# Recurrent mixer: V's second tile and token shift placed behind the keys, and the low-rank weights loaded ahead of V's

## The chip, the core and the metric

The kernel runs on one core of a Trainium2 chip. The core has five engines with queues of their own: TensorE (PE, with its weight loads shown as PEld), VectorE (DVE), ScalarE (ACT), GpSimd (POOL) and SyncE (SP, which here only issues DMAs). Each queue is worked off in order, and instructions wait for other engines on semaphores. The metric is the device time of one execution in microseconds.

## The reference

Two layers on 256 tokens of width 1024. Each layer is a SwiGLU block, a mixer and a second SwiGLU block, each between two RMS norms. Layer 0 has the mixer in question, layer 1 an attention mixer. What matters here, cut from the reference:

```python
p = proj[..., :COLS_RWKV]
p_prev = jnp.pad(p, ((0, 0), (1, 0), (0, 0)))[:, :-1]
p = p + shift_mu * (p_prev - p)                     # token shift
r, k, v, d_w, d_a, d_g = split_cols(p, [...])
decay = exp(-exp(-softplus(-(decay_base + tanh(d_w) @ decay_up)) - 0.5))
a = sigmoid(iclr_base + d_a @ iclr_up)              # low-rank parts
g = sigmoid(d_g) @ gate_up
kk = normalised(k * k_k);  k = k * (1 + (a - 1) * k_a)
# per token: S = S diag(w) - (S kk)(kk a)^T + v k^T ;  y = S r
y_b = silu(layer_norm(conv(c_val * sigmoid(c_gate)) + conv_b))
return concat([y_a, y_b]) @ w_out
```

## The kernel before

All tokens are held as two tiles of 128 (t = 0, 1). Every float32 product is made of three passes with operands split into a high and a low part. A weight page of 128x1024 floats is loaded by SP into one of 10 `raw` buffers; `split` (L97) then casts it on ScalarE into `whi` (L98) and forms `wlo = raw - whi` on VectorE or, for the names in `POOLED` (among them `av`, `alora`, `ak`, `ar`, `ao0`), on GpSimd (L99). There are 8 `whi` and 8 `wlo` buffers; a page is taken in the order in which `plan` (L1034) has added it.

The stages are SwiGLU, recurrent mixer, two SwiGLUs, attention, SwiGLU. The recurrent mixer, `mixer_a` (L564), calls its parts in the order of the letters in `ORDER` (L22), "VLDKPQkRIBCcbA2nS". Those that matter here:

- V, `values` (L603): for each token tile the product with `av` (24 matmuls 128x512, by `xunit`, L338), its scaling into `pv` on ScalarE (L615), and DMAs from ScalarE's queue that copy `pv` down by one row into `prev` (L618, L620). Between the tiles `across` (L377) makes `rb`, the row scale for products that stand transposed. Then, for each tile, the token shift on GpSimd (L622 to L624), the mean over 64 columns on VectorE (L626, L627) and its subtraction into `vz` on GpSimd (L630). `vz` is first read by the state stage.
- L, `lora` (L641): the product with `alora` (48 matmuls 128x256, by `wunit`, L352), its shift (`shifted`, L632: `n` on VectorE at L635, ScalarE at L638, VectorE at L639), tanh and sigmoid, and the small products that give `sg`, `ic` and `gg`.
- D, `decay` (L667): `restart` set by GpSimd (L671, L672), a scan on VectorE (L674), `epx` on GpSimd (L676), exponentials on ScalarE.
- K, `keys` (L661): two products of 48 matmuls and their shift. P, Q: `bk`, `ur` and the matrix `Q` (L730, 16 instructions on VectorE).
- I, `invert` (L732): `Q` goes to DRAM and back (L740, L746), a chain of small VectorE instructions inverts 16x16 blocks (L749 to L773), and the results go to DRAM and back as `G` and `T`.
- C, `glu` (L834): two gated products; `z` on VectorE (L845), its sigmoid on ScalarE (L846), `glu` on VectorE (L847). c, `conv`: diagonal weights `dw` on ScalarE (L906), taps on VectorE (L926, `feed`), on GpSimd (L915) and on TensorE (`pfeed`, `gu<-glu,dw`).
- A, 2, S: `ak` and `ar` (L818, L821), the doubling of `G` and `T`, and the state over four chunks.

This call order sets priorities; the order on each engine is laid down by a scheduler when the kernel is built. `issue_after` keeps an instruction behind another in that order.

Of the kernel before, what the change touches and what calls it, by code (L numbers as in the profile page):

```python
# [12 lines left out]
ALU = mybir.AluOpType  # L13
PSUM = bass.MemoryType.PSUM
P = 128
D = 1024
# [2 lines left out]
TAG = dict(sq8="y2", qn="yc", gz="z", fz="tmp", fe="c16", fl="lora", fc="n", fraw="restart", pt="yb", y="muv",  # L19
           cb="ur", cbm="bk", gt="sg", qt="ic", kt="k", v="vz", y0="ar")  # L20

ORDER = "VLDKPQkRIBCcbA2nS"  # L22

NRAW, NWEIGHT, NAHEAD = 10, 8, 8

# [67 lines left out]
class Kernel:  # L93
# [470 lines left out]
    def mixer_a(self, j, rstd, nxt, then):  # L564
        nc, W, a = self.nc, self.w, self.a
        V = nc.vector
# [15 lines left out]
        m = {}  # L582
# [8 lines left out]
        muv = self.temp("muv", [512])  # L591
# [11 lines left out]
        def values():  # L603


            vz = m["vz"] = [half(self.page("vz")) for _ in range(2)]
            pv, prev = m["v"], _ = half(self.page("pv")), half(self.page("prev"))
            W.upto(("av",))
            with self.tc.issue_after(self.pow.ins):
                nc.gpsimd.memset(prev[0:1, 0, :], 0.0)  # L610
            for t in range(2):
                if t:
                    m["rb"] = self.across(rstd)
                ps = self.xunit(("av",), t)
                nc.scalar.activation(pv[:, t, :], ps, AF.Copy, scale=rstd[t])  # L615

                for a, b in ((0, 112), (112, P - 1)):
                    nc.scalar.dma_start(out=prev[a + 1:b + 1, t, :], in_=pv[a:b, t, :])  # L618
                if t == 0:
                    nc.scalar.dma_start(out=prev[0:1, 1, :], in_=pv[P - 1:P, 0, :])  # L620
            for t in range(2):
                nc.gpsimd.tensor_tensor(out=prev[:, t, :], in0=prev[:, t, :], in1=pv[:, t, :], op=ALU.subtract)  # L622
                m["shift"] = nc.gpsimd.tensor_tensor(out=prev[:, t, :], in0=prev[:, t, :], in1=muv, op=ALU.mult)
                nc.gpsimd.tensor_tensor(out=pv[:, t, :], in0=prev[:, t, :], in1=pv[:, t, :], op=ALU.add)  # L624
                v8 = self.small("v8", 8)
                V.tensor_reduce(out=v8, in_=h8(pv[:, t, :]), axis=AX.X, op=ALU.add)  # L626
                V.tensor_scalar(out=v8, in0=v8, scalar1=1.0 / 64, scalar2=None, op0=ALU.mult)  # L627
                for c in range(2):
                    cs = slice(64 * c, 64 * c + 64)
                    nc.gpsimd.tensor_tensor(out=h8(vz[t][cs, c, :]), in0=h8(pv[cs, t, :]), in1=v8[cs].unsqueeze(2).broadcast_to([64, 8, 64]), op=ALU.subtract)  # L630
# [36 lines left out]
        def decay():  # L667
            sg = m["sg"]
            restart = self.temp("restart", [1024], BF16)
            with self.tc.issue_after(m["shift"].ins):  # L670
                nc.gpsimd.memset(restart, 1.0)  # L671
                nc.gpsimd.memset(restart.rearrange("p (n t) -> p n t", t=64)[:, :, 0:1], 0.0)  # L672
            dc = self.page("dc")
            V.tensor_tensor_scan(out=dc, data0=restart, data1=flat(sg), initial=0.0, op0=ALU.mult, op1=ALU.add)  # L674
            epx = self.page("epx")
            nc.gpsimd.tensor_tensor(out=epx, in0=dc, in1=flat(sg), op=ALU.subtract)  # L676
            nc.scalar.activation(epx, epx, AF.Exp, scale=-DEC)
            ep = self.page("ep")
            nc.scalar.activation(ep, dc, AF.Exp, scale=-DEC)
            nc.scalar.activation(dc, dc, AF.Exp, scale=DEC)  # L680
            m["epx"], m["ep"], m["en"] = grp(epx), grp(ep), grp(dc)
# [286 lines left out]
        def state():  # L968
# [4 lines left out]
            for ch in range(4):  # L973
# [44 lines left out]
                    ts = slice(t * P, (t + 1) * P)  # L1018
                    self.split(self.xth[:, 0:4, ts], self.xtl[0][:, :, ts], tp.rearrange("p (g t) -> p g t", t=P))

        f = {"V": values, "L": lora, "K": keys, "D": decay, "P": prep, "k": kprep, "Q": qmats, "I": invert, "R": receptance, "A": amats,
             "B": kback, "C": glu, "2": doubling, "b": bonus, "c": conv, "n": convend, "S": state}
        for z in ORDER:
            f[z]()
# [9 lines left out]
    def plan(self, stages):  # L1034
        W, a = self.w, self.a
        flat = lambda ap: ap.rearrange("p k f -> p (k f)")
        for st in stages:
            if st in "0134":
                j = int(st)
                l, f = j // 3, j % 3  # L1040
                units = self.units()
                for i, u in enumerate(units + [None] * 2):
# [7 lines left out]
                    if i >= 2:  # L1050
                        v = units[i - 2]
# [1 line left out]
                            if ("d", j, v[1], k) not in W.where:  # L1053
                                W.add(("d", j, v[1], k), a["wd"][l, f, v[1], :, k], 1024)
            if st == "A":
                for name in [n for z in ORDER for n in dict(V=["av"], L=["alora"], K=["ak"], R=["ar"], C=["acv", "acg"]).get(z, [])]:
                    if name == "av":
                        for h in range(2):
                            W.add((name,), flat(a["av"][h]), 512)
                        continue  # L1060
                    o, n = {"ak": (0, 4), "ar": (4, 4), "acv": (8, 4), "acg": (12, 4), "alora": (16, 2)}[name]
                    for g in range(o, o + n):
                        W.add((name,), flat(a["ain"][g]), 128)
                for h in (2, 3, 0, 1):
                    W.add(("ao", h // 2), flat(a["aout"][h]), 1024)
# [10 lines left out]
    def run(self, out):  # L1076
        tc, nc, a = self.tc, self.nc, self.a
        self.turn = 0
        with tc.tile_pool(name="c", bufs=1) as c, tc.tile_pool(name="raw", bufs=NRAW) as raw, tc.tile_pool(name="pg") as pg, \
# [26 lines left out]
            nc.sync.dma_start(out=self.x[1], in_=a["x"][P:2 * P, :])  # L1106
            order = "0A13C4"
            rstd = {t: self.pre(t, order.index(self.stages[0])) for t in range(2)}
            first = lambda st: {"A": [("av",), ("alora",)], "C": [("q", 0), ("k", 0)]}.get(st) or [("g", int(st), 0), ("g", int(st), 1)]
            for n, st in enumerate(self.stages):  # L1110
                nx = self.stages[n + 1] if n + 1 < len(self.stages) else None
                f = getattr(self, {"A": "mixer_a", "C": "mixer_c"}.get(st, "ffn"))
# [85 lines left out]
```

## Time and profile before

| what | value |
| --- | --- |
| three runs | 1122.84, 1125.05, 1146.17 us; median 1125.05 us |
| the profiled execution | 1123.03 us, of which 1121.2 us is the span from first to last instruction |
| busy in the span | PE 96%, PEld 84%, DVE 60%, ACT 51%, POOL 23% |
| the recurrent mixer | from about 207 us to about 386 us of the span |

A row of the timeline reads: start and duration in us, engine, line, operation, output<-inputs, count, and in brackets how long the engine had been idle before it and what ended that. "SPq" and "ACTq" are a queue's DMA issues. In a list of waits the columns are the engine and line that waited, whom it waited for, us in total, number of times and the longest. A row of the stretches gives the busy time of each engine in it, the TensorE clock that was granted (1.00 is 2.4 GHz, 0.50 is 1.2 GHz), the busy share of the DMA engines and GB/s.

### The profile page before, as it was taken

Reading aid. Unit: us, or ns where it says so; the run is one execution under the profiler, and the core shown is the slowest. Engines: PE = TensorE matmul, PEld = TensorE weight load, DVE = VectorE, ACT = ScalarE, POOL = GpSimd, SP = SyncE. Lnnn points to the kernel's source line nnn. Section 1 sums busy time; section 2 is a strip of 40 time slices with the busy share of each in tenths; the row PEclk is TensorE's granted clock in tenths of the full one; section 3 lists DMA queues with packets and bytes.
Section 4 is the critical chain, followed back from the end, with each engine's and each line's share of the span. In section 5 each row is a group of like instructions: output and inputs, shape, how many; then the busy total and the mean of one; then the engine's idle time right before and its main releaser. Section 6 shows DMA issues by size and latency. Waiting matters only on the chain.

```text
span 1121.2 us, 17652 instructions
## 1 busy us (share of the span) xinstructions
PE 1075.6 (96%) x6955; PEld 947.1 (84%) x6955; DVE 668.3 (60%) x1064; ACT 568.5 (51%) x933; POOL 255.1 (23%) x194
## 2 busy tenths in 40 slices
PE   7999999999698899999989999999999989999997
PEld 5899998889587789999878999988887868999986
DVE  4465661599887556547444555836667665555722
ACT  7444553673453464446354544634666945444611
POOL 4200006571662170000070000001564540000000
PEclk9999999998798999999999999999999999999999
DMA  9766785245410246557554464744273553765400
GB/s 361 246 212 185 235 308 177 86 165 151 104 39 1 76 151 244 201 189 271 168 186 151 167 227 170 240 138 151 90 286 107 193 189 101 226 193 179 148 1 37
DMA packets 65321, 189.27 MB, mean 169 GB/s; under 512 B 18360, under 2 KB 19672, under 8 KB 65238
## 3 DMA queue, kind: packets, MB, share of 16 engines
q1 hardware_dynamic: 55386, 186.18, 49.4%
q10 hardware_dynamic: 9852, 1.96, 1.0%
q8 instruction: 54, 0.88, 0.3%
q14 instruction: 29, 0.24, 0.1%
HBM read 184.68 MB, written 2.92 MB: 167 GB/s over the span
## 4 chain that ended last, share of the span: by engine, by line
PE 66%; DVE 7%; ACT 2%; DMA 1%; issue 1%; POOL 1%; ACTq 0%; DVEq 0%; POOLq 0%
PE gu L352 23%; PE acc L263 16%; PE gu L223 12%; PE gu L338 5%; PE acc L370 3%; PE gu L585 2%; PE acc L585 2%; DVE cv L926 2%; DVE wlo L99 1%; DVE x L148 1%; PE tr L158 1%; POOL p L484 1%; PE tr L506 1%; ACT whi L98 0%; DMA raw<-in_cout_dram 0%
## 5 line engine op out<-in xcount | busy, mean ns | idle before, releaser
L98 ACT CAST whi<-raw 128x1024 fp32r<-128x1024 f32 x294 | 303.4, 1047 | 206.2 <-PE gu L352 110.8
L99 DVE TENSOR_TENSOR wlo<-raw,whi 128x1024 fp32r<-128x1024 f32 x248 | 312.5, 1266 | 133.9 <-ACT whi L98 108.1
L352 PE MATMUL gu<-xth,wlo 128*128 128x256 f32 x1104 | 314.1, 284 | 0.0
L352 PE MATMUL gu<-xl,whi 128*128 128x256 f32 x1104 | 313.1, 284 | 0.0
L352 PE MATMUL gu<-xth,whi 128*128 128x256 f32 x1104 | 313.1, 284 | 0.0
L352 PEld LDWEIGHTS gu<-xth,wlo 128*128 128x128 f32 x1104 | 212.0, 192 | 3.5 <-issue 0.9
L352 PEld LDWEIGHTS gu<-xth,whi 128*128 128x128 f32 x1104 | 211.8, 192 | 3.3 <-issue 0.7
L352 PEld LDWEIGHTS gu<-xl,whi 128*128 128x128 f32 x1104 | 211.9, 192 | 1.0 <-issue 0.8
L99 POOL TENSOR_TENSOR wlo<-raw,whi 128x1024 fp32r<-128x1024 f32 x46 | 113.9, 2506 | 300.1 <-PE gu L223 141.5
L263 PE MATMUL acc<-whi,ht 128*128 128x512 f32 x576 | 168.0, 393 | 0.0
L113 POOL TENSOR_TENSOR misc<-misc 128x1 f32<-128x1 f32 (+1 forms) x36 | 31.6, 880 | 476.0 <-DVE misc L130 380.7
L263 PEld LDWEIGHTS acc<-whi,ht 128*128 128x128 f32 x576 | 104.0, 189 | 18.3
L263 PE MATMUL acc<-wlo,ht 128*128 128x512 f32 x288 | 89.9, 392 | 0.0
L234 DVE TENSOR_TENSOR h<-gu,h 128x256 f32<-128x256 f32 x88 | 36.9, 420 | 77.9 <-ACT h L230 74.7
L232 DVE TENSOR_TENSOR h<-gu,misc 128x256 f32<-128x256 f32 x56 | 23.7, 424 | 80.1 <-PE gu L352 80.1
L223 PE MATMUL gu<-whi,xth 128*128 128x512 f32 x160 | 63.8, 403 | 1.8 <-ACT whi L98 1.8
L223 PE MATMUL gu<-wlo,xth 128*128 128x512 f32 x160 | 64.0, 400 | 0.5 <-DVE wlo L99 0.5
L263 PEld LDWEIGHTS acc<-wlo,ht 128*128 128x128 f32 x288 | 53.9, 188 | 11.8
L223 PE MATMUL gu<-whi,xl 128*128 128x512 f32 x160 | 63.3, 400 | 0.1
L233 ACT ACTIVATE h<-h 128x256 f32<-128x256 f32 x56 | 23.2, 415 | 53.7 <-DVE h L232 53.7
L230 ACT ACTIVATE h<-gu,misc 128x256 f32<-128x256 f32 x32 | 15.1, 475 | 66.9 <-PE gu L223 36.9
L338 PE MATMUL gu<-whi,xth 128*128 128x512 f32 x112 | 44.9, 401 | 1.1 <-ACT xth L162 0.9
(254 smaller groups left out, 1589.6 us busy)
## 6 DMA issues: line engine op xcount, KB each, us to landing
raw<-in_wgc_dram SPq DMA_DIRECT2D x112, 512.0 KB, 4.5
raw<-in_wd_dram SPq DMA_DIRECT2D x88, 512.0 KB, 4.7
raw<-in_wgt_dram SPq DMA_DIRECT2D x64, 512.0 KB, 5.3
raw<-in_cin_dram SPq DMA_DIRECT2D x24, 512.0 KB, 5.2
raw<-in_ain_dram SPq DMA_DIRECT2D x18, 512.0 KB, 4.5
raw<-in_aout_dram SPq DMA_DIRECT2D x8, 512.0 KB, 5.1
raw<-in_cgate_dram SPq DMA_DIRECT2D x8, 512.0 KB, 7.5
raw<-in_cout_dram SPq DMA_DIRECT2D x8, 512.0 KB, 3.7
```

The lines of the kernel that those rows point to most:

```text
L98: self.nc.scalar.copy(out=hi, in_=raw)
L99: (engine or self.nc.vector).tensor_tensor(out=lo, in0=raw, in1=hi.bitcast(F32), op=ALU.subtract)
L113: self.pow = self.nc.gpsimd.tensor_tensor(out=out, in0=v, in1=self.mhalf[:, :n], op=ALU.pow)
L223: nc.tensor.matmul(ps, lhsT=l, rhs=r[:, k % 2], start=n == 0, stop=n == 23)
L232: nc.vector.tensor_tensor(out=z, in0=ps[:, 0:256], in1=self.rb, op=ALU.mult)
L233: nc.scalar.activation(sl, z, AF.Silu)
L234: nc.vector.tensor_tensor(out=h, in0=ps[:, 256:512], in1=sl, op=ALU.mult)
L263: mm = nc.tensor.matmul(out, lhsT=l, rhs=r, start=u[1] == 0 and i + n == 0, stop=u[1] == NB - 1 and i * 3 + n == 5)
L338: self.nc.tensor.matmul(ps, lhsT=l, rhs=r[:, k % 2], start=n == 0, stop=n == 23)
L352: self.nc.tensor.matmul(ps[:, j * 256:(j + 1) * 256], lhsT=l, rhs=r, start=n == 0, stop=n == 23)
L370: self.nc.tensor.matmul(accs[t][c], lhsT=l, rhs=r[:, 0, c * 512:(c + 1) * 512], start=k == ks[0] and n == 0, stop=k == ks[7] and n == 2)
L585: return nc.tensor.matmul(out, lhsT=lhsT, rhs=rhs, start=start, stop=stop, skip_group_check=True)
```

## The change

V's first tile, with `across`, stays where it was. The product of the second tile and the whole token shift become a part of its own, "v", called behind P. The pages of `alora` are planned, and taken at the end of the SwiGLU before, ahead of those of `av`. `restart` is held only behind the last `pow` of the norm, no longer behind the shift. Lines behind L611 move by about five.

```diff
-ORDER = "VLDKPQkRIBCcbA2nS"
+ORDER = "VLDKPvQkRIBCcbA2nS"
...
-            for t in range(2):
-                if t:
-                    m["rb"] = self.across(rstd)
+
+            def product(t):
                 ps = self.xunit(("av",), t)
                 nc.scalar.activation(pv[:, t, :], ps, AF.Copy, scale=rstd[t])
...
+            product(0)
+            m["rb"] = self.across(rstd)
+            m["rest"] = lambda: (product(1), shift_values(vz, pv, prev))
+
+        def shift_values(vz, pv, prev):
             for t in range(2):
                 nc.gpsimd.tensor_tensor(out=prev[:, t, :], in0=prev[:, t, :], in1=pv[:, t, :], op=ALU.subtract)
-                m["shift"] = nc.gpsimd.tensor_tensor(out=prev[:, t, :], in0=prev[:, t, :], in1=muv, op=ALU.mult)
+                nc.gpsimd.tensor_tensor(out=prev[:, t, :], in0=prev[:, t, :], in1=muv, op=ALU.mult)
...
-            with self.tc.issue_after(m["shift"].ins):
+            with self.tc.issue_after(self.pow.ins):
                 nc.gpsimd.memset(restart, 1.0)
...
-        f = {"V": values, "L": lora, ...
+        f = {"V": values, "v": lambda: m["rest"](), "L": lora, ...
...
-                for name in [n for z in ORDER for n in dict(V=["av"], L=["alora"], K=["ak"], R=["ar"], C=["acv", "acg"]).get(z, [])]:
+                for name in [n for z in ORDER for n in dict(V=["alora", "av"], K=["ak"], R=["ar"], C=["acv", "acg"]).get(z, [])]:
...
-            first = lambda st: {"A": [("av",), ("alora",)], "C": [("q", 0), ("k", 0)]}.get(st) or [("g", int(st), 0), ("g", int(st), 1)]
+            first = lambda st: {"A": [("alora",), ("av",)], "C": [("q", 0), ("k", 0)]}.get(st) or [("g", int(st), 0), ("g", int(st), 1)]
```

The orders differ only inside the recurrent mixer (and in three places of SP's loads around it). At its start TensorE had, behind the transposes of the second token tile (`x_75`), V's second product (L338) interleaved with the low-rank product (L352):

```order
L158 MATMUL tr<-cst,x_75 128x128 x8
L338 MATMUL gu<-whi,xth 128x512
L338 MATMUL gu<-wlo,xth 128x512
L352 MATMUL gu<-xth,whi 128x256
L352 MATMUL gu<-xth,wlo 128x256
L338 MATMUL gu<-whi,xl_88 128x512
L352 MATMUL gu<-xl_88,whi 128x256
L338 MATMUL gu<-whi,xth 128x512
```

Now the low-rank product stands there alone:

```order
L158 MATMUL tr<-cst,x_75 128x128 x8
L352 MATMUL gu<-xth,whi 128x256
L352 MATMUL gu<-xth,wlo 128x256
L352 MATMUL gu<-xth,whi 128x256
L352 MATMUL gu<-xth,wlo 128x256
L352 MATMUL gu<-xl_88,whi 128x256 x2
```

V's 24 matmuls come behind both products of the keys. On GpSimd, at the same place, the row was this before; `wlo` are weight pages, `prev`, `pv` and `vz` the shift of V's tiles:

```order
L610 MEMSET prev 1x512
L622 TENSOR_TENSOR prev<-prev,pv 128x512
L623 TENSOR_TENSOR prev<-prev,muv 128x512
L99 TENSOR_TENSOR wlo<-raw,whi 128x1024
L624 TENSOR_TENSOR pv<-prev,pv 128x512
L99 TENSOR_TENSOR wlo<-raw,whi 128x1024 x2
L630 TENSOR_TENSOR vz<-pv,misc 64x512 x2
L99 TENSOR_TENSOR wlo<-raw,whi 128x1024 x2
L622 TENSOR_TENSOR prev<-prev,pv 128x512
L99 TENSOR_TENSOR wlo<-raw,whi 128x1024
L623 TENSOR_TENSOR prev<-prev,muv 128x512
L671 MEMSET restart 128x1024
```

and is this now:

```order
L610 MEMSET prev 1x512
L676 MEMSET restart 128x1024
L677 MEMSET restart 128x16
L627 TENSOR_TENSOR prev<-prev,pv 128x512
L628 TENSOR_TENSOR prev<-prev,muv 128x512
L629 TENSOR_TENSOR pv<-prev,pv 128x512
L635 TENSOR_TENSOR vz<-pv,misc 64x512 x2
L99 TENSOR_TENSOR wlo<-raw,whi 128x1024 x5
L681 TENSOR_TENSOR epx<-dc,sg 128x1024
L99 TENSOR_TENSOR wlo<-raw,whi 128x1024
L627 TENSOR_TENSOR prev<-prev,pv 128x512
L628 TENSOR_TENSOR prev<-prev,muv 128x512
```

The first tile's shift is done in one go ahead of the weight pages, the second tile's stands behind `epx`. On VectorE, at the end of `Q`, the row was

```order
L730 SCALAR_TENSOR_TENSOR Q<-acc_2417,misc,cst 128x64
L730 SCALAR_TENSOR_TENSOR Q<-acc_2418,misc,cst 128x64
L635 TENSOR_TENSOR n<-gu,misc 128x512
L99 TENSOR_TENSOR wlo<-raw,whi 128x1024 x2
L639 SCALAR_TENSOR_TENSOR r<-n,cst,r 128x255 x2
```

and is

```order
L735 SCALAR_TENSOR_TENSOR Q<-acc_2417,misc,cst 128x64
L631 TENSOR_REDUCE misc<-pv 128x8
L735 SCALAR_TENSOR_TENSOR Q<-acc_2418,misc,cst 128x64
L99 TENSOR_TENSOR wlo<-raw,whi 128x1024
L644 SCALAR_TENSOR_TENSOR r<-n,cst,r 128x255 x2
```

so the sum over the second tile of V, which waits for GpSimd, stands between the last two of the 16 instructions that make `Q`. On VectorE, from the first taps of the convolution to the second `glu`, the row was

```order
L926 SCALAR_TENSOR_TENSOR cv<-glu,cst,cv 128x255 x2
L818 TENSOR_TENSOR ak<-acc_3054,cst 64x4x64
L821 TENSOR_TENSOR ar<-acc_3054,cst 128x4x64
L926 SCALAR_TENSOR_TENSOR cv<-glu,cst,cv 128x254 x2
L845 TENSOR_TENSOR z<-gu,misc 128x512
L818 TENSOR_TENSOR ak<-acc_3055,cst 64x4x64
L821 TENSOR_TENSOR ar<-acc_3055,cst 128x4x64
L818 TENSOR_TENSOR ak<-acc_3073,cst 64x4x64
L926 SCALAR_TENSOR_TENSOR cv<-glu,cst,cv 128x253 x2
L818 TENSOR_TENSOR ak<-acc_3074,cst 64x4x64
L818 TENSOR_TENSOR ak<-acc_3092,cst 64x4x64
L847 TENSOR_TENSOR glu<-cv,z 128x512
```

and is

```order
L931 SCALAR_TENSOR_TENSOR cv<-glu,cst,cv 128x255 x2
L850 TENSOR_TENSOR z<-gu,misc 128x512
L823 TENSOR_TENSOR ak<-acc_3054,cst 64x4x64
L826 TENSOR_TENSOR ar<-acc_3054,cst 128x4x64
L931 SCALAR_TENSOR_TENSOR cv<-glu,cst,cv 128x254 x2
L823 TENSOR_TENSOR ak<-acc_3055,cst 64x4x64
L826 TENSOR_TENSOR ar<-acc_3055,cst 128x4x64
L823 TENSOR_TENSOR ak<-acc_3073,cst 64x4x64
L852 TENSOR_TENSOR glu<-cv,z 128x512
```

with the second `z` one pair of taps earlier, and one pair of taps and two `ak` fewer ahead of the second `glu`.

## Rows read from the trace of the kernel before

**Rows 1.** The stretch 180 to 440 us in steps of ten, sum row: busy us by engine.
```profile
sum 260.00, PE 237.29 PEld 206.07 DVE 182.96 ACT 133.82 POOL 122.95; mean PE 9.13 PEld 7.93 DVE 7.04 ACT 5.15 POOL 4.73
```

**Rows 2.** Whom TensorE waited for between 190 and 420 us.
```profile
PE gu L585 <- ACT dw L906: 8.5, 1, 8.5
PE acc L585 <- DVE bk L693: 3.4, 1, 3.4
PE acc L585 <- DVE ar L821: 2.3, 1, 2.3
```

**Rows 3.** Whom VectorE waited for between 228.3 and 304.1 us.
```profile
DVE glu L847 <- ACT z L846: 2.9, 1, 2.9
DVE wlo L99 <- ACT whi L98: 1.1, 2, 0.9
```

**Rows 4.** Timeline of VectorE.
```profile
212.40 0.61 DVE L163 SCALAR_TENSOR_TENSOR xl<-tr,cst,xth 128x128 fp32r<-128x128 f32 x2 [0.85 <-ACT xth L162]
...
228.32 0.69 DVE L635 TENSOR_TENSOR n<-gu,misc 128x512 f32<-128x512 f32 x1 [0.53 <-PE gu L352]
...
231.05 4.03 DVE L639 SCALAR_TENSOR_TENSOR k<-n,cst,k 128x255 f32<-128x255 f32 x2
...
239.72 0.67 DVE L626 TENSOR_REDUCE misc<-pv 128x8 f32<-128x512 f32 x1
...
261.22 3.14 DVE L730 SCALAR_TENSOR_TENSOR Q<-acc,misc,cst 128x64 f32<-128x64 f32 x16
...
266.99 1.23 DVE L99 TENSOR_TENSOR wlo<-raw,whi 128x1024 fp32r<-128x1024 f32 x1 [0.90 <-ACT whi L98]
268.13 0.88 DVE L639 SCALAR_TENSOR_TENSOR r<-n,cst,r 128x255 f32<-128x255 f32 x2
...
273.15 0.43 DVE L749 TENSOR_TENSOR inv<-inv,c 128x256 f32<-128x256 f32 x1
...
295.75 4.15 DVE L926 SCALAR_TENSOR_TENSOR cv<-glu,cst,cv 128x254 f32<-128x254 f32 x2
...
301.65 0.86 DVE L926 SCALAR_TENSOR_TENSOR cv<-glu,cst,cv 128x253 f32<-128x253 f32 x2
302.43 0.87 DVE L818 TENSOR_TENSOR ak<-acc,cst 64x256 f32<-64x256 f32 x2
303.33 0.69 DVE L847 TENSOR_TENSOR glu<-cv,z 128x512 f32<-128x512 f32 x1
```

**Rows 5.** Timeline of TensorE.
```profile
198.87 0.39 PE L338 MATMUL gu<-whi,xth 128*128 128x512 f32 x1
...
215.31 0.39 PE L338 MATMUL gu<-wlo,xth 128*128 128x512 f32 x1
215.54 0.39 PE L338 MATMUL gu<-whi,xl 128*128 128x512 f32 x1
...
217.86 0.28 PE L352 MATMUL gu<-xth,whi 128*128 128x256 f32 x1
217.98 0.28 PE L352 MATMUL gu<-xth,wlo 128*128 128x256 f32 x1
...
304.17 3.45 PE L585 MATMUL gu<-glu,dw 128*128 128x255 f32 x8 [8.51 <-ACT dw L906]
```

**Rows 6.** Timeline of GpSimd.
```profile
177.72 14.20 POOL L99 TENSOR_TENSOR wlo<-raw,whi 128x1024 fp32r<-128x1024 f32 x6 [6.03 <-PE acc L263]
...
230.00 2.27 POOL L622 TENSOR_TENSOR prev<-prev,pv 128x512 f32<-128x512 f32 x1
```

**Rows 7.** Groups on GpSimd, 228.3 to 304.1 us: count, then busy us and mean ns.
```profile
L99 POOL TENSOR_TENSOR wlo<-raw,whi 128x1024 fp32r<-128x1024 f32 x6 | 17.1, 2851 | 0.0
```

**Rows 8.** Timeline of ScalarE.
```profile
238.91 1.28 ACT L679 ACT_TABLE_LOAD   x1
242.63 1.06 ACT L679 ACTIVATE ep<-dc 128x1024 f32<-128x1024 f32 x1 [2.44 <-DVE dc L674]
```

**Rows 9.** DMA issues between 205 and 235 us: KB each, median us from issue to landing.
```profile
prev<-pv ACTq DMA_DIRECT2D x2, 224.0 KB, 2.7
```

More of the change, by code (lines that the diff above doesn't have):

```diff
@@ L1019, in state @@
                     self.split(self.xth[:, 0:4, ts], self.xtl[0][:, :, ts], tp.rearrange("p (g t) -> p g t", t=P))
-        f = {"V": values, "L": lora, "K": keys, "D": decay, "P": prep, "k": kprep, "Q": qmats, "I": invert, "R": receptance, "A": amats,
+        f = {"V": values, "v": lambda: m["rest"](), "L": lora, "K": keys, "D": decay, "P": prep, "k": kprep, "Q": qmats, "I": invert, "R": receptance, "A": amats,
              "B": kback, "C": glu, "2": doubling, "b": bonus, "c": conv, "n": convend, "S": state}
```

## The prediction, made before the changed kernel was run

> **What bounds the kernel now.** I read the stretches first. Over the 260 us from 180 to 440, which hold the whole mixer, TensorE is busy for 237.29 [rows 1], so it has at most 260 − 237.29 = 22.7 us to give there, and outside the mixer the change touches nothing. That caps any gain at about 2% of the kernel, which is also about what a measurement of this kernel can tell from no change.
>
> The list of TensorE's waits says where part of this stands: 8.5 us before `dw`, 3.4 before `bk`, 2.3 before `ar` [rows 2]. The longest ends at 304.17, where the convolution's products start [rows 5]. `dw` is named as releaser, but on VectorE the second `glu` runs 303.33 + 0.69 = 304.02 [rows 4], and these products read `glu` as well. I take VectorE's `glu` as the real gate.
>
> So I walked VectorE backwards from there. The timeline between the keys' `n` at 228.32 and 304.02 is nearly unbroken: 2.9 us behind the sigmoid of `z`, 1.1 behind casts [rows 3], and nothing else long. In these 304.02 − 228.32 = 75.7 us VectorE is the bound of the mixer, and TensorE fills in beside it or waits. At the left end the row reverses: `n` had been waited for from TensorE (0.53 idle behind `gu`) [rows 4]. The chain is therefore TensorE up to 228.32, VectorE for 75.7 us, TensorE from 304.17.
>
> **The change part by part.**
>
> V's second product leaves the head of this chain. Its matmuls follow each other by 215.54 − 215.31 = 0.23 us, the low-rank ones by 217.98 − 217.86 = 0.12 [rows 5]. The last `xl` of the second token tile is there at 212.40 + 0.61 = 213.0 [rows 4]; what reads it can't run earlier. Before, 24 matmuls of V and 48 of the low-rank product shared the time up to about 221.2 us, as the keys' n at 228.32 less 48 matmuls of 0.12 and a few small products shows (228.32 − 5.8 = 222.5). In the new order 22 of the 48 stand before the first ones that read the late `xl_89`, so 26 are left at 213.0: 213.0 + 26 × 0.12 + about 0.3 for the two transposes among them = 216.4. Then 48 of the keys' first half, 5.8 us, give `n` at about 222.2: **6.1 us earlier**. The price is TensorE's fill from 208 to 213: eleven matmuls of V (0.23) stood there and eleven of 0.12 now do, so about 1.2 us of idle that is on no path, as VectorE's work for these tiles sets the 213.0.
>
> The order of loading costs nothing. Six GpSimd casts end at 177.72 + 14.20 = 191.92 [rows 6], 7 us ahead of V's first matmul at 198.87 [rows 5], now the later reader. Were this cover gone, two casts of 14.20 / 6 = 2.4 would cost 4.8.
>
> VectorE's 75.7 us change in three ways.
> - Work: the new order has two taps (0.86) and two `ak` (0.87) fewer ahead of the second `glu`, and one weight split more (1.23 alone) [rows 4]: −0.5. The sum over V (0.67) is moved, not added.
> - Waits: with work taken from between, VectorE comes sooner to things that ScalarE makes. I count the table load that now stands ahead of the keys (1.28, with the wait of an ACTIVATE behind it about 1.5), the scan without the 0.67 sum ahead of it (0.7), and `misc<-ep`, which waits for a load of 1.28 and `ep` of 1.06 less one `n` of 0.69 (1.7) [rows 4, 8]. That is 3.9; the 1.1 behind casts [rows 3] goes. Net +2.8. Bounds: 1, if only the last wait appears beyond what goes, and 6, if all of 3.9 and about as much as the worst ScalarE gap again (2.44, ahead of `ep` [rows 8]) come.
> - Slowing beside GpSimd: a pair of taps takes 4.15 us while GpSimd casts and 0.86 when it does not, the pair for `k` 4.03 against 0.88 for `r` [rows 4]. Six casts of 2.85, 17.1 us, stand in this stretch [rows 7]. V's first tile now goes ahead of the casts, so that roughly 3.8 us more of casting (one and a third of 2.85) falls beside the keys, after one late cast that goes behind the convolution is deducted. At half inflation I take +1.9; bounds 0 (all of it falls beside VectorE work that reads PSUM: the 16 of `Q` take 0.2 each in any case) and 3.
>
> The Trainium skill, page "SBUF — State Buffer", section "Who interferes with whom", says that a VectorE instruction with two SBUF inputs and a GpSimd instruction that reads SBUF exclude each other for a whole instruction, while one SBUF input is harmless. The pair 4.15 against 0.86 agrees [rows 4]. It speaks against this change: by it V's second shift, five GpSimd instructions, would block VectorE for up to their whole duration (by its row of 2.27 [rows 6], an estimate of some 8 us for five) if they met splits and `bk`, and the sum would come out at a loss; they also leave the keys, where they blocked `k` before, and I cancel the two.
>
> Sum: 75.7 − 0.5 + 2.8 + 1.9 = 79.9. From 222.2 this gives `glu` at 302.1 and the convolution's products at about 302.3 against 304.17: **−1.9 us**. TensorE reaches `Q`'s products sooner, so the 3.4 before `bk` shrinks, but it then waits for VectorE further down; I book nothing. V's 24 matmuls (5.5 us) fill TensorE while VectorE does the gates: no cost. The memset of `restart` goes to a gap of GpSimd, and SP's one load that moves past `Q`'s DMA is no longer than another: 0. Behind 302 the work is the same.
>
> The profiled execution took 1123.03 us (span 1121.2 and 1.8 around it), 2 below the median of the three runs, 1125.05. 1123.03 − 1.9 = **1121** is my forecast.
>
> **Rivals.**
>
> *VectorE sheds its waits.* If casts and shifts rarely meet VectorE's splits, and ScalarE keeps ahead, the stretch stays near 75.7 − 0.5 + 0.5 and the whole 6.1 arrives: −6.1 to −8, counting the 2.9 behind the sigmoid [rows 3] partly gone because `z` comes one pair of taps earlier. About 1115.5. For it: most of VectorE's stretch is its own busy time, which just shifts. Against it: every earlier start of VectorE meets a ScalarE and a GpSimd that did not start earlier by as much.
>
> *The sum over V blocks `Q`* (the slower side). It stands ahead of the last of `Q`'s 16 instructions and waits for GpSimd. V's product ends at about 222.2 + 5.8 (keys) + 5.5 (V) + 5.7 (small products) = 239. `pv` waits for ScalarE, whose exponentials then run (`ep` at 242.63 [rows 8]), and its copy takes 2.7 us [rows 9]: about 249. Three GpSimd instructions of 1.3 to 2.3 and a cast of 2.85 [rows 6, 7]: 256. `Q`'s fifteenth instruction comes at 261.22 + 2.9 [rows 4] before, and some 2 to 5 us earlier now: 259 to 262. There are thus 3 to 6 us of slack. If two more casts slip in (5.7) and ScalarE is late, the sum ends near 264, `Q` about 5 us late, the inversion (which started at 273.15, held by the round trip through DRAM) with it, and −1.9 turns into about +2.5: 1125.5. It decides from the point where GpSimd's addition ends behind `Q`'s fifteenth.
>
> *Nothing at the end.* If VectorE meets all that I have bounded above (waits 6, slowing 3 less 0.5) the stretch grows by what the head gave, 6.1 to 8: the convolution starts where it did, and the time is 1123 to 1125.
>
> **How the numbers follow.** Forecast 0.4, shed waits 0.25, nothing at the end 0.2, blocked `Q` 0.15. The range runs from 1112, a little under the shed waits, to 1128, over the blocked `Q` with the upper bounds. A gain of over 2%, 22.5 us, would need nearly all of TensorE's 22.7 idle us: 0.03. A loss of over 2% would need the blocked `Q` four times over: 0.03. The rest, 0.94, is within 2%.
>
> **What would show it.** In the changed profile the keys' first `n` should start near 222 and what holds it should still be TensorE (at 226 or later the head's term is wrong). `Q`'s instructions should end near 259 without a wait for GpSimd at the sum over V; the inversion start near 267 to 269; the second `glu` end near 302 (297: first rival; 306: second, and then the list of VectorE's waits shows that sum waiting for `pv`). V's 24 matmuls should stand without a gap between the keys and the small products. The wait of TensorE at the convolution should be longer than 8.5 where the sum is right, since its own work is done sooner. The forecast is wrong as a whole if the waits shift to the state stage behind 310 us, which I left unchanged.

## The result, and the profile after

The changed kernel took 1139.2 us (median) against 1125.42 for the kernel before on the same chip: 1.0121 times as long, 95% interval 1.0086 to 1.0156, about 13.6 us. The forecast was 1121, its range 1112 to 1128: the sign was wrong, and the time lies outside, though within the 2% that had the chance of 0.94. Executions in which TensorE runs all or most of the doubling (the stage behind the convolution's start) at half clock occur with most kernels here and are some 20 us longer (the kernel before: 1144 to 1148); the comparisons leave them out, but e5, e7, e8, e10 and e12 had no others, so their ratios set half clock against full.

The profiled execution took 1136.12 us, its span is 1134.3: 13.1 more than before. The change adds and removes almost no instructions, so I follow landmarks through the two traces. First VectorE, at the head of the mixer and from the inversion to the second `glu` (start, us, engine, line, operation, count, idle before):

```profile
219.32 0.69 DVE L640 TENSOR_TENSOR n<-gu,misc 128x512 f32<-128x512 f32 x1 [2.22 <-PE gu L352]
221.58 3.46 DVE L644 SCALAR_TENSOR_TENSOR lora<-n,cst,lora 128x255 f32<-128x255 f32 x2 [1.57 <-ACT lora L643]
224.96 0.68 DVE L640 TENSOR_TENSOR n<-gu,misc 128x512 f32<-128x512 f32 x1
...
258.39 2.95 DVE L735 SCALAR_TENSOR_TENSOR Q<-acc,misc,cst 128x64 f32<-128x64 f32 x15
261.26 0.67 DVE L631 TENSOR_REDUCE misc<-pv 128x8 f32<-128x512 f32 x1
...
273.34 0.43 DVE L754 TENSOR_TENSOR inv<-inv,c 128x256 f32<-128x256 f32 x1 [3.35 <-DMA inv<-dq]
...
304.73 0.68 DVE L852 TENSOR_TENSOR glu<-cv,z 128x512 f32<-128x512 f32 x1
```

The keys' `n` starts at 224.96, 3.4 us earlier than before [rows 4], with no wait for TensorE. The second `glu` ends at 305.41, 1.4 later than before. GpSimd shows why the sum over V (261.26) had no wait, and where the convolution's additions end:

```profile
219.80 9.99 POOL L99 TENSOR_TENSOR wlo<-raw,whi 128x1024 fp32r<-128x1024 f32 x4
...
256.76 2.16 POOL L629 TENSOR_TENSOR pv<-prev,pv 128x512 f32<-128x512 f32 x1
...
331.36 2.21 POOL L920 TENSOR_TENSOR cv<-cz,cv 128x241 f32<-128x241 f32 x3 [9.55 <-ACT cz L919]
334.81 2.35 POOL L99 TENSOR_TENSOR wlo<-raw,whi 128x1024 fp32r<-128x1024 f32 x1 [1.25 <-PE acc L585]
...
354.04 0.58 POOL L920 TENSOR_TENSOR cv<-cz,cv 128x226 f32<-128x226 f32 x1
```

The last addition ends at 354.62. Before, it ended at 341.38:

```profile
340.64 0.74 POOL L915 TENSOR_TENSOR cv<-cz,cv 128x226 f32<-128x226 f32 x1
```

TensorE from the convolution to the end of the mixer, after:

```profile
305.55 1.19 PE L585 MATMUL gu<-glu,dw 128*128 128x255 f32 x2 [1.11 <-ACT dw L911]
306.67 1.97 PE L585 MATMUL gu<-vz,ak 64*64 64x64 f32 x16
308.57 2.90 PE L585 MATMUL gu<-glu,dw 128*128 128x254 f32 x6
311.40 2.47 PE L585 MATMUL acc<-T,Q 64*64 64x64 f32 x32
...
354.94 0.44 PE L943 MATMUL tr<-cst,cv 128*128 128x128 f32 x2 [1.62 <-DVE cv L968]
...
358.24 1.12 PE L956 MATMUL tr<-cst,xc 128*128 128x128 f32 x4 [1.02 <-DVE xc L953]
359.15 1.06 PE L943 MATMUL tr<-cst,cv 128*128 128x128 f32 x4
360.14 1.97 PE L585 MATMUL acc<-R,G 64*64 64x64 f32 x16
364.25 1.12 PE L585 MATMUL acc<-vz,kb 128*64 128x64 f32 x16 [2.14 <-DVE vz L993]
...
396.43 0.66 PE L158 MATMUL tr<-cst,x 128*128 128x128 f32 x4 [1.78 <-DVE x L148]
```

and the same places before:

```profile
348.99 1.03 PE L585 MATMUL acc<-R,G 64*64 64x64 f32 x14
...
352.20 0.69 PE L585 MATMUL acc<-vz,kb 128*64 128x64 f32 x16 [0.79 <-DVE vz L988]
...
385.52 0.96 PE L158 MATMUL tr<-cst,x 128*128 128x128 f32 x4 [2.10 <-DVE x L148]
```

Two orders changed here, and neither is near the code that moved. (`R,G` is the product with which a chunk of the recurrence begins; `vz,ak`, `vz,kb` and `T,Q` are others of its small products.) The eight products of the convolution with which TensorE comes back [rows 5] are split: two, sixteen small ones (`vz,ak`), six. And the transposes of the convolution's norm (L943, L956), which wait for GpSimd's additions through `cv`, now stand ahead of `R,G`, the first step of the second chunk of the recurrence. The lateness grows like this: +1.1 where the mixer begins, +1.4 at the restart (305.55 against 304.17), +3.1 at the first `T,Q` (308.31 before), +12.1 at the second chunk's `vz,kb` (364.25 against 352.20), +10.9 at the end of the mixer. So restart to end takes 396.43 − 305.55 = 90.88 us instead of 81.35. The remaining 2.2 come later, in code that the change doesn't touch. The 1.1 at the start says little: over all traces here the mixer begins between 196.8 and 198.4, without a pattern.

The granted clock of the stretches (us, then busy us and count of PE, PEld, DVE, ACT, POOL, then PEclk, DMA share, GB/s), after and then before:

```profile
300.00:310.00 10.00, 8.56 (x46) 7.27 (x46) 9.84 (x21) 7.30 (x22) 3.73 (x3) 0.50 0.16 48
310.00:320.00 10.00, 9.15 (x102) 7.49 (x101) 6.66 (x12) 8.18 (x21) 7.52 (x12) 0.87 0.00 0
```
```profile
300.00:310.00 10.00, 5.83 (x56) 4.96 (x56) 9.66 (x24) 9.46 (x30) 0.35 (x1) 0.64 0.01 2
310.00:320.00 10.00, 9.22 (x114) 7.78 (x113) 5.85 (x9) 7.01 (x15) 8.98 (x14) 1.00 0.01 2
```

After, the clock was back at its upper level (2.4 GHz, 1.00) between 312 and 313 us, 7 us behind the restart; before, it was back between 307 and 308, 3 us behind it.

### The profile page after: what moved, and what is told of

Read it like the earlier page. It is cut to its first block, busy times and chain, and to the rows that moved or that the text cites. A ratio compares the mean times of both kernels' runs of the same rounds, so it can differ in the third digit from the quotient of the medians.

```text
span 1134.3 us, 17641 instructions
## 1 busy us (share of the span) xinstructions
PE 1083.3 (96%) x6955; PEld 953.6 (84%) x6955; DVE 668.2 (59%) x1064; ACT 568.7 (50%) x933; POOL 258.2 (23%) x194
## 4 chain that ended last, share of the span: by engine, by line
PE 84%; DVE 7%; ACT 3%; POOL 2%; issue 2%; DMA 1%; ACTq 0%; SPq 0%; DVEq 0%; POOLq 0%
PE gu L352 32%; PE acc L263 21%; PE gu L223 16%; PE gu L338 4%; PE acc L370 3%; PE acc L585 2%; PE gu L585 2%; DVE x L148 1%; DVE cv L931 1%; DVE wlo L99 1%; PE tr L158 1%; DMA raw<-in_wgt_dram 1%; ACT whi L98 1%; POOL p L484 1%; PE tr L243 1%
## 5 line engine op out<-in xcount | busy, mean ns | idle before, releaser
L99 DVE TENSOR_TENSOR wlo<-raw,whi 128x1024 fp32r<-128x1024 f32 x248 | 309.2, 1254 | 145.1 <-ACT whi L98 122.3
L352 PE MATMUL gu<-xth,whi 128*128 128x256 f32 x1104 | 313.7, 284 | 1.4 <-ACT xth L162 1.3
L352 PE MATMUL gu<-xth,wlo 128*128 128x256 f32 x1104 | 313.8, 284 | 0.0
L352 PE MATMUL gu<-xl,whi 128*128 128x256 f32 x1104 | 313.4, 284 | 0.0
L352 PEld LDWEIGHTS gu<-xth,whi 128*128 128x128 f32 x1104 | 212.5, 193 | 5.0 <-ACT xth L162 2.0
L352 PEld LDWEIGHTS gu<-xth,wlo 128*128 128x128 f32 x1104 | 212.6, 193 | 2.6 <-issue 0.3
L352 PEld LDWEIGHTS gu<-xl,whi 128*128 128x128 f32 x1104 | 212.4, 193 | 1.2 <-issue 1.0
L99 POOL TENSOR_TENSOR wlo<-raw,whi 128x1024 fp32r<-128x1024 f32 x46 | 111.6, 2456 | 304.9 <-PE gu L223 142.2
L338 PE MATMUL gu<-whi,xth 128*128 128x512 f32 x112 | 44.7, 399 | 1.6 <-ACT v L423 1.6
```

The lines of the kernel that those rows point to most:

```text
L99: (engine or self.nc.vector).tensor_tensor(out=lo, in0=raw, in1=hi.bitcast(F32), op=ALU.subtract)
L338: self.nc.tensor.matmul(ps, lhsT=l, rhs=r[:, k % 2], start=n == 0, stop=n == 23)
L352: self.nc.tensor.matmul(ps[:, j * 256:(j + 1) * 256], lhsT=l, rhs=r, start=n == 0, stop=n == 23)
```

## The experiments

### What the order of the second chunk costs: e1 to e4

e1 gives the transposes of the convolution's norm a place behind `R,G` of the second chunk:

```diff
-            for t in range(2):
-                conv_norm(t)
...
                     i = mm(pz[zs, h, :], G[zs, t, h, :], R[zs, t, h * 64:h * 64 + 64])
+                if ch == 1:
+                    for z in range(2):
+                        conv_norm(z, i)
```

with `issue_after` of that matmul around the transposes; the taking of the next weight pages (`W.upto`) moves with them. e2 puts the weight split of GpSimd that stands at 334.81 behind its last addition (`issue_after`). e3 does both. e4 does the reverse to the kernel before: `R,G` of the second chunk is issued behind the second tile's transposes, and nothing else changes.

> The changed kernel, with one edit: the norm of the convolution (its transposes, L943 and L956) is issued behind the second chunk's products R x G of the state. Theory A (order in the state): the mixer lost 9.5 us because TensorE now has the convolution's transposes ahead of the second chunk (R x G at 360.1 instead of 349.0 us), and the state waits for a convolution that ends at 354.1. Then R x G comes at about 353, the kernel gets 4 to 7 us shorter than the changed one (about 1132 to 1135), and the rest of the loss stays. Theory B (the convolution's end sets the end in any order, as the output product reads it first): 0 to 1 us, about 1138 to 1139. Theory C (the clock at half rate around 300 to 311 us and the later doubling are the loss): 0.

One comparable execution: 1135.03, against 1136.12 to 1139.76 for the change.

> The changed kernel, with one edit: the fourth weight split of ao0 on GpSimd stands behind the last addition of the convolution there, not among them (where it took 2.35 us, 1.25 us of wait and the place of one addition after the other). Theory A: the additions end some 3 us earlier, the transposes and with them the second chunk too: 2 to 3 us shorter than the changed kernel, about 1136. Theory D (this split is the cause of the loss): 6 us or more, about 1132. Theory C: 0.

One comparable execution: 1133.16, some 5 us less than the change and more than I expected of this edit.

> Both edits of the two runs before it. Theory A: the two overlap, 5 to 7 us shorter than the changed kernel, about 1132 to 1134. Theory B: as the second edit alone, 2 to 3 us, about 1136. Theory C: 0, about 1139.

Measured 1129.42 to 1130.87, ratio to before 1.0055 [1.0033, 1.0076]: the two together bring back 7.4 of the 13.6 us. How the 7.4 divides between them isn't shown: e1 and e2 have one comparable execution each.

> The kernel before, with one edit: the products R x G of the state's second chunk are issued behind the first transposes of both tiles of the convolution's norm, as they stand in the changed kernel. Theory A: R x G moves from 349.0 to behind the transposes of xc, which stand at 353.8, and the kernel gets 4 to 6 us longer than before, about 1129 to 1131; that it is less than in the changed kernel is because the convolution ends at 346.8 here, 7 us earlier. Theories B and C: 0 to 1 us, about 1125.

Measured 1129.89 to 1132.05, 1.0054 [1.0035, 1.0073]: the order alone costs the kernel before 6.1 us. TensorE in e4:

```profile
350.03 0.91 PE L938 MATMUL tr<-cst,cv 128*128 128x128 f32 x4 [0.30 <-DVE cv L926]
...
353.70 0.63 PE L951 MATMUL tr<-cst,xc 128*128 128x128 f32 x4 [1.27 <-DVE xc L948]
...
354.69 1.14 PE L585 MATMUL acc<-R,G 64*64 64x64 f32 x16
359.22 1.12 PE L585 MATMUL acc<-vz,kb 128*64 128x64 f32 x16 [3.38 <-DVE vz L989]
```

`R,G` waits out the norm's chain between two sets of transposes, as in the changed kernel, and `vz,kb` is 7.0 us later than before. Of these, 1.8 were there at the restart (306.00), in an order that e4 leaves alone; from the restart to the end of the mixer e4 takes 87.58 us, the kernel before 81.35. These 6.2 are the price of the order. That settles the largest part: a serial chain (`R,G`, then `vz`, then `vz,kb`) stands behind work that nobody needs yet.

### The loads and the places of V: e5 to e8

```diff
e5, on e3:  -ORDER = "VLDKPvQkRIBCcbA2nS"   +ORDER = "VLDKPvQkRIiBCcbA2nS"
            (i: the inversion from L754 on, issued behind r's second half)
e6, after:  -V=["alora", "av"]   +V=["av", "alora"]   (and in first())
e7, before: -V=["av"], L=["alora"]   +V=["alora", "av"]   (and in first())
e8, after:  -ORDER = "VLDKPvQkRIBCcbA2nS"   +ORDER = "VvLDKPQkRIBCcbA2nS"
```

> The changed kernel with the old order of the pages (av ahead of alora in the plan and at the end of the SwiGLU before); the instructions stand in the same order otherwise. Theories A and E: the order of the loads is no part of the loss: within 1.5 us of the changed kernel, 1137 to 1140. Rival G (the low-rank pages ahead make V's first product late: it comes 1.1 us later in the changed profile): 1 to 3 us shorter, 1135 to 1137.

Measured 1.0131 [1.0108, 1.0154], as the change itself: the order of loading plays no part in the loss as a whole.

> The changed kernel with the two edits of the third run and one more: VectorE's first instruction of the inversion (L754, which waits for the DMA) is issued behind the second half of r (L644), not ahead of it. Theory E (VectorE's order): in the changed kernel r's second half waits with VectorE for that DMA until 273.3 us, so GpSimd's r x k starts at 275.3 instead of 269.2, the chain of Wg and gg ends at 303.3 instead of 294.6, and dw waits for it. With the edit gg ends some 4 to 6 us earlier, dw at 301 to 302, and the kernel gets 2 to 4 us shorter than the third run's 1130.4, about 1127. Rival F (that chain is late but VectorE's second glu sets the restart anyway): 0 to 1 us, about 1130.

Measured 1.0178 [1.0158, 1.0198].

> The kernel before with the new order of the pages alone. It moves the second glu on VectorE ahead of a pair of taps and several ak, and one weight split of ao0 on GpSimd from ahead of the convolution's additions to behind them. Theory A: no loss of the changed kernel comes from here; 0 to 3 us shorter than before, 1122 to 1125, as the second glu comes earlier. Rival G: 1 to 3 us longer, about 1127.

Measured 1.0191 [1.0156, 1.0226].

> The changed kernel with the part v called right behind V: V's second tile and its shift in their old place, the new order of the pages and the freed restart kept. Two weight splits of ao0 stand among GpSimd's additions, and the state's second chunk stands ahead of the convolution's transposes. Theory A: the loss of the changed kernel comes from order behind 290 us, which V's move only set off: here the two splits cost 2 to 5 us on the convolution's end and nothing stands behind it, so 1125 to 1130. Rival H (V's product behind the keys itself costs the time, as fill that TensorE lacks at 208 to 213 and as work added later): 1125 or less, the whole 13 us back.

Measured 1.0196 [1.0173, 1.0218]. I had foreseen no such loss for any of these three. In all of them the convolution starts earlier than before (301.24, 303.12, 299.20), and the kernel is 20 us longer. Two stretches of e7:

```profile
330.00:340.00 10.00, 10.00 (x72) 8.31 (x71) 4.72 (x11) 0.00 (x0) 0.00 (x0) 0.50 0.00 0
340.00:350.00 10.00, 10.00 (x73) 8.32 (x71) 5.79 (x10) 5.75 (x12) 5.88 (x9) 0.50 0.01 2
```

TensorE is busy for all of both, and the clock stays at its lower level (1.2 GHz, 0.50) from 300 to 360. These 20 us are not a slower kernel: the kernel before takes as long, 1144 to 1148, where its own doubling runs at half clock, and what e5, e7 and e8 would take at full clock isn't shown. By their times the three had half clock in twelve executions out of twelve, the kernel before in 10 of 68. What they share is how TensorE came back from the wait: not with eight `glu,dw` together but with 6, 16 small, 2 (e5), with 4, 16 small, 2, 8 small, 2 (e8), and in e7:

```profile
303.12 2.88 PE L585 MATMUL gu<-glu,dw 128*128 128x255 f32 x6 [2.70 <-DVE glu L847]
...
307.93 1.21 PE L585 MATMUL gu<-glu,dw 128*128 128x252 f32 x2
```

with eight small ones (`ur,bk`) between.

### The eight products held together: e9 to e12

e9 (on after), e10 (on e7) and e11 (on e5) keep the eight together: all four taps are fed behind the fourth block of scores, not one behind each block, and `vz,ak` of the first chunk is issued behind the eighth.

```diff
-                pfeed(PFEED[0], i)
+                if ch == 3:
+                    pfeed(4 * PFEED[0], i)
...
+                    with self.tc.issue_after(burst.ins) if ch == 0 else contextlib.nullcontext():
                         mm(py[zs, h, :], ak[cs, t, h * 64...
```

e12 does the reverse to the kernel before: the last four of `ur,bk` are issued behind the third tap, so that its eight break into 6 and 2 with eight small ones between.

> The changed kernel, with one edit: the four taps of the convolution on TensorE (eight matmuls) that open the restart stand together, ahead of the 16 small products vz x ak, as in the kernel before (there: eight matmuls, 3.45 us, and the granted clock is back at 1.00 behind them). Theory K (the bunch of dense matmuls is what brings the clock back; in the changed kernel two of them, 16 small products and then six stand there, and the clock is back some 4 us later): full rate from about 309 instead of 312, 2 to 3 us shorter than the changed kernel, about 1135 to 1136. Rival L (the clock comes back by itself some time after the stall, whatever the order): 0 to 1 us, about 1138.

Measured 1.0093 [1.0075, 1.0111], about 3 us less than the change; the intervals overlap. Keeping the eight together does not make sure of the clock: the profiled execution (1157.08) has them in one piece (3.72 us) and 0.50 behind them, to 370.

> The kernel before with the new order of the pages (the seventh run, 1145) and with the eight matmuls together, behind the last product ur x bk, where that run had six, then eight products ur x bk, then two, and a clock of 0.50 from 300 to 360 us. Theory K: the clock is back at 1.00 by about 310, the 20 us go: 1122 to 1126. Rival L: nothing changes, 1143 to 1147, and another thing in the order of that run holds the clock down.

Measured 1.018 [1.0163, 1.0197]: no gain. But the trace shows something other than in e7:

```profile
310.00:320.00 10.00, 6.91 (x100) 5.98 (x99) 9.96 (x16) 6.61 (x14) 9.06 (x13) 1.00 0.00 0
320.00:330.00 10.00, 10.00 (x71) 8.24 (x69) 6.99 (x13) 1.08 (x3) 3.17 (x5) 0.50 0.01 2
```
```profile
318.96 2.58 PE L585 MATMUL acc<-G,WT 64*64 64x64 f32 x32 [3.09 <-DVE WT L868]
...
323.42 3.31 PE L585 MATMUL acc<-WT,G 64*64 64x64 f32 x32
```

The eight brought the clock to 1.00, then TensorE waited 3.09 us for VectorE's `WT`, and from there the clock is 0.50 to 360.

> The fifth run (the changed kernel with its three edits, 1144; the convolution's products start at 301.2 us, six matmuls, then 16 small ones, then two; clock 0.50 up to 365 us) with the eight matmuls together. Theory K: clock back by 306, 18 to 22 us shorter than the fifth run: 1120 to 1126, as the three edits have taken back what the order cost and V's product is behind the keys. Rival L: 1143 to 1145.

Measured 1.0071 [1.0053, 1.0089], 12 us less than e5, with the convolution at 302.43: less than the 18 to 22 I expected, as the clock came back here but did not stay. It was at 1.00 from 310 to 320, and behind a wait of 2.38 for `T` at 329.84 it is 0.50; a wait of 3.88 for `WT` follows. What VectorE did ahead of them:

```profile
319.64 8.95 DVE L942 SCALAR_TENSOR_TENSOR cv<-glu,cst,cv 128x244 f32<-128x244 f32 x12
...
329.71 8.53 DVE L942 SCALAR_TENSOR_TENSOR cv<-glu,cst,cv 128x238 f32<-128x238 f32 x9
338.17 0.68 DVE L882 TENSOR_TENSOR WT<-acc,cst 128x512 f32<-128x512 f32 x1
```

Twelve and nine taps of the convolution between two steps of the doubling, 0.75 and 0.95 us each while GpSimd adds, where a tap takes 0.43 alone [rows 4].

> The kernel before, with one edit: the last four products ur x bk (eight matmuls of 128x64) stand between the third and the fourth tap, so that the bunch of eight is broken into six and two, as in the seventh run. With it the scheduler also puts the first transposes of the convolution's norm ahead of the state's second chunk, which was worth 6 us in the fourth run. Theory K: clock 0.50 through the doubling, 1143 to 1150. Rival L: 1130 to 1132, what the transposes alone cost.

Measured 1.0198 [1.0177, 1.0219], and the clock 0.50 from 300 to 360. In this build the norm's transposes also moved ahead of the second chunk, which cost 6.1 us in e4. That doesn't show here: e12's 1145 to 1150 us are about what the kernel before takes at half clock. What the broken eight brought is half clock as the rule, in four executions out of four.

### All cured: e13 to e17

e13 is e3 with the eight together. e14 is e11, and e15 e10, with fewer taps between two steps of the doubling (`FEED`: 4, 3, 12 becomes 4, 3, 6 in e14 and 3, 3, 12 in e15). e16 is e8 (V's second tile directly behind the first) with the eight together, both edits of e3 and `FEED` 3, 3, 8. e17 is the kernel before with the eight held together, the transposes behind `R,G`, `FEED` 4, 3, 6, and the last taps on VectorE called behind the first chunk's `vz`.

> The changed kernel with the state's second chunk ahead of the convolution's transposes, the split of ao0 behind the additions, and the eight matmuls together. If the three causes add up, the third run's 1130.4 less the 2 to 3 us of the ninth: 1127 to 1129. If the bunch gives nothing beside the two other edits: 1130 to 1131.

Measured 1.004 [1.0021, 1.0058]. From the restart to the end of the mixer its trace takes 82.15 us, against 90.88 for the change and 81.35 before: the cures return 8.7 of the 9.5 us lost there.

> The eleventh run (1132) with 6 instead of 12 taps of VectorE fed behind each G and T of the doubling. There nine to twelve taps took 8.5 to 9.0 us beside GpSimd's additions, TensorE waited 2.4 us for T and 3.9 for WT, and its clock fell to 0.50 from 330 to 355 us. Theory M (a wait of over 3 us in the doubling drops the clock, and small products don't bring it back): no such wait, clock 1.00 from 306 on, 8 to 12 us shorter, 1120 to 1124, that is as the kernel before or shorter. Rival N (the small products alone lose the clock in the end): clock 0.50 again, 1129 to 1132.

Measured 1.0015 [1.0003, 1.0027], a little over the 1120 to 1124 expected; the clock is 1.00 from 310 to 340, without a wait of over 1 us there. The 3 us in the expectation are no limit that a run shows: in e11 0.50 followed a wait of 2.38.

> The tenth run (1145) with three instead of four taps fed behind each chunk of ak and ar, so that six instead of nine taps (7.2 us there) stand on VectorE ahead of the first WT, for which TensorE waited 3.1 us at 319. Theory M: TensorE waits about 1 us there, the clock stays at 1.00: 18 to 22 us shorter, 1122 to 1127. Rival N: 1143 to 1146.

Measured 1.0022 [1.0012, 1.0032] over seven executions (1126 to 1127); the other three took 1148 to 1149, and e10's four 1143 to 1147. So with fewer taps full clock was the rule, but not certain. The profile is of one of the three, and there the eight together were followed by half clock, with no wait of over 1 us behind them up to 340:

```profile
303.27 3.72 PE L585 MATMUL gu<-glu,dw 128*128 128x255 f32 x8 [3.18 <-DVE glu L849]
...
310.00:320.00 10.00, 9.22 (x63) 7.33 (x60) 4.79 (x7) 5.99 (x12) 8.90 (x15) 0.50 0.00 0
```

> The eighth run (V's second tile and shift in their old place, new order of the pages, freed restart; 1146, its convolution's products started at 299.2 us, six us ahead of the fourteenth run's, but with the clock at 0.50 through the doubling) with the cures: eight matmuls together, the state's second chunk ahead of the convolution's transposes, the last split of ao0 behind the additions, 3 taps fed behind each chunk and 8 behind each G and T. If the move of V is worth nothing in the end: 1118 to 1124, shorter than the kernel before. If the move gains its 4 us of the head also at the end: longer than the fourteenth run, 1127 to 1131.

Measured 1122.78 us (median), 0.9986 [0.9972, 1.0].

> The kernel before with the state's second chunk ahead of all of the convolution's transposes, and 6 instead of 12 taps fed behind each G and T; the eight matmuls stand together there anyway. VectorE's wait ahead of G at 340 us (1.7 us of TensorE) goes, and the second chunk comes 0.6 us earlier: 1121 to 1124, 1 to 3 us shorter than before; if the convolution's later end takes it back: 1124 to 1126.

Measured 1.0006 [0.9996, 1.0017]: the cures are worth nothing to the kernel before, whose order had neither fault. TensorE in e16, the fastest kernel of the study:

```profile
300.67 3.18 PE L590 MATMUL gu<-glu,dw 128*128 128x255 f32 x8
...
383.40 0.60 PE L163 MATMUL tr<-cst,x 128*128 128x128 f32 x4
```

It restarts 3.5 us earlier than before and ends the mixer 2.1 earlier, but its interval reaches 1.0. With V's second tile behind the keys the best result is 1.0015 (e14), with V in its old place 0.9986: no build shows a gain from the move of V at the end, even where its side effects are cured. A price for the move alone these two don't give, as they differ also in `FEED` and in the place of the inversion.

## Why the prediction was wrong

**The step that failed** is "Behind 302 the work is the same". The work was the same, its order was not. With the moved part the scheduler gave other places to code that I took as unchanged (how it came to them no run shows); the orders that I set side by side ahead of the prediction end at the second `glu`, and they differ to the end of the mixer. Of the 13.1 us in the trace, 9.5 arose between the restart and the end of the mixer. e3 takes back 7.4 with two edits behind 305, e4 produces 6.1 in the kernel before with one, and e13 returns 8.7 of the 9.5. The prediction's last sentence names waits that shift to the state stage as what would make it wrong as a whole; I gave that neither a price nor a chance.

**The rest of the 13.6.** Of the 6.2 that e3 leaves, holding the eight together (e13) takes 1.7 (1.0055 to 1.004, intervals overlapping). Most of what e13 leaves is in the attention stage. Between the first transposes of `x` at 781.44 and 935.05 the changed kernel takes 153.6 us, before 150.5 (770.77 to 921.23), and TensorE waits 1.6 for ScalarE's `v` (L423) and 1.0 more for `x`, with TensorE, VectorE, ScalarE and GpSimd in the same order of instructions. This is no chance of one execution: the stage takes 153.6 in the traces of e1, e2, e3, e5, e9, e11 and e13 to e16 too, and 150.4 to 150.5 in e4 and e12. e15 and e16, where V stands in its old place, have it as well, so V's move alone is not the cause. The loads have a part in it: e6, which differs from the change in the order of the pages alone, takes 154.9, and e7 151.9. The rest stays open.

**The head, −6.1, was mis-sized: −3.4.** The prediction let VectorE wait for TensorE at the keys, but `n` started without a wait for it, behind the pair for `lora` on VectorE. That pair was late: the low-rank products were forecast to end at 216.4, and `n` of `alora` came at 219.32, behind a wait for TensorE. And it was slow: 3.46 us beside GpSimd's four splits (219.80 to 229.79), where it took 1.68 before and the pair for `r` takes 0.88 [rows 4]:

```profile
222.79 1.68 DVE L639 SCALAR_TENSOR_TENSOR lora<-n,cst,lora 128x255 f32<-128x255 f32 x2 [0.73 <-ACT lora L638]
```

The Trainium skill's page "SBUF — State Buffer", section "Who interferes with whom", has these two kinds of instruction exclude each other, and 3.46 against 0.88 agrees. I used that rule for V's shift and the casts beside the keys, and not for the splits that the shift now lets through ahead of them.

**VectorE's stretch, 75.7 to 79.9, came to 80.45 (224.96 to 305.41) by luck.** The stretch before and after (the third number pair from the left of each row is VectorE's):

```profile
228.32:304.02 75.70, 61.31 (x536) 57.40 (x534) 71.07 (x111) 34.99 (x56) 40.48 (x23) 0.89 0.53 138
224.96:305.41 80.45, 72.06 (x552) 65.98 (x551) 66.96 (x109) 39.73 (x63) 45.70 (x22) 0.88 0.54 153
```

VectorE was idle for 80.45 − 66.96 = 13.5 us instead of 4.6: 8.9 more, where the forecast had 2.8 and an upper bound of 6. It was busy for 4.1 less, where the forecast had work and slowing at 1.4 more. The two errors nearly cancel. The wait for ScalarE's `ep` came (1.88); the 3.35 for DMA at the inversion and 1.77 for `ic` were not booked.

**Inversion at 267 to 269: wrong, 273.34.** `Q` ended at 262.1, 2.2 earlier than before, but the round trip through DRAM that follows took 11.2 us instead of 8.8 and gave that back. Over all traces it takes 8.3 to 13.9 from the end of `Q` to the inversion's first instruction; in e1, e2 and e3, whose edits all lie behind it, it took 11.3, 11.0 and 13.5, so part of it varies from execution to execution. The second half of `r` (274.28) stands behind that wait on VectorE, so GpSimd's `r`×`k` (275.32), its chain for `gg` and ScalarE's `dw` came late as well. e5 moved `r` ahead, and its restart came at 301.24.

***The sum over V blocks Q* did not happen.** GpSimd's addition ended at 256.76 + 2.16 = 258.92, and `Q`'s fifteenth instruction at 261.3: 2.3 us of slack, below the 3 to 6 I allowed. *VectorE sheds its waits* fell with the stretch. *Nothing at the end* came nearest: counted from the start of the mixer the restart is 0.3 later than before. Its sizes were others (the stretch grew by 4.8 and the head gave 3.4), and its time, 1123 to 1125, failed by what came behind the restart. No rival had the clock or the order behind 302 in it.

**The wait before `dw`,** said to grow beyond 8.5, was 1.1. An order of TensorE that I had not followed to its end put a wait of 2.9 for `z` and others ahead of it:

```profile
PE acc L585 <- DVE vz L993: 5.7, 2, 3.6
PE acc L585 <- DVE z L850: 2.9, 1, 2.9
PE tr L585 <- POOL sq L798: 2.8, 1, 2.8
...
PE gu L585 <- ACT dw L911: 1.1, 1, 1.1
```

**The loads at nothing** were right for the changed kernel (e6). Alone on the kernel before they gave 2% (e7), by way of the order behind the restart and the half clock in the doubling, not of the loading: e15 has the same loads at 1.0022.

## What to carry to other kernels

Where a scheduler sets the order, compare the orders of all engines to the end of the stage before calling the code behind the change unchanged, and look first for low-priority work with a long wait (here a norm) that has slipped ahead of a serial chain. Behind a long wait of TensorE, keep its dense products together and keep the other engines from making it wait again; here that raised the share of executions at full clock and did not make sure of it. A gate passed 3 us earlier is worth nothing if the stretch behind it runs at half the clock.

## What the runs showed of the hardware

The same stream of 64x64 products ran at either clock: 32 of `G,WT` took 1.90 us at 1.00 (before) and 3.31 at 0.50 (e1). How it was entered decided this in part.

- After eight dense products in one piece (3.2 to 3.7 us) the clock was 1.00 in the next ten microseconds, or nearly so, in the traces of before, e4, e10, e11, e13, e14, e16 and e17. In those of e9 and e15 it stayed at 0.50 behind the same eight.
- After two, sixteen small and six it was back within 10 us of the restart in after and e6, and stayed at 0.50 in e1, e2 and e3.
- After six or four, small ones, and the rest in twos it stayed at 0.50 in all four traces (e5, e7, e8, e12). By their times all sixteen executions of these builds ran so, against 9 of 21 with two, sixteen, six, and 21 of 129 with the eight together (e10 not counted).

So the order moves the odds, and what decides a single execution isn't shown. At 0.50 TensorE was busy for 10.00 of 10 us with small products and four dense ones at a time, and the clock did not rise (e7, 330 to 350); entered at 1.00, the same products kept it (e14, 310 to 340). The Trainium skill, page "TensorE: Matmul & The Clock Gate", section "What's actually happening", says that activity releases the throttle. The recoveries behind dense products agree; e7, e9 and e15 show that being busy in the records was not enough. A wait of 3.09 us (e10) and one of 2.38 (e11) were followed by 0.50.
